# Hymba block on one core: half of the output weights split during attention and kept in DRAM, the gate's operands placed in weight buffers that are no longer used

## The chip, the cores and the metric

The kernel runs on one core of one Trainium2 chip. The metric is the device time of one execution in microseconds (us). The kernel before took 2211.99 us, the median of three runs (2210.46 to 2216.73).

## The reference

One layer of a streaming encoder, 2048 tokens of 1024 features in float32. A normalised input is projected once; 512 columns feed a state-space layer, the rest are q, k, v of a chunked attention with 8 heads. Both results are normalised, joined, and sent through one output projection; a SwiGLU feed-forward layer follows.

```python
h = rmsnorm(x, norm_mix_g[l])
proj = h @ w_in[l]
...
y = jax.nn.gelu(y.reshape(bsz, seq, D_SSM))
y = y * jax.nn.sigmoid(y @ w_glu.astype(f32) + b_glu.astype(f32))
...
y_att = chunked_attention(q, k, v, attn_rel_bias[l])
mixed = jnp.concatenate([rmsnorm(y_ssm, norm_ssm_out_g[l]),
                         rmsnorm(y_att, norm_att_out_g[l])], axis=-1)
x = x + mixed @ w_out[l]
h2 = rmsnorm(x, norm_ffn_g[l])
x = x + (jax.nn.silu(h2 @ w_gate[l]) * (h2 @ w_up[l])) @ w_down[l]
return rmsnorm(x, norm_final_g)
```

## The kernel before

**Precision.** Nearly every product is made of three matmuls (`mm3`): each float32 operand is split into a rounded part and a rest (`split`, L177 to L179). ScalarE (ACT) casts the rounded part, VectorE (DVE) subtracts it, so a split is one instruction on each of the two engines, the second waiting for the first. Names such as `gh`/`gl` or `woh`/`wol` are the two parts of one operand.

**Stages.** After a prologue (state-space layer, first projections) the attention runs as 130 steps in four blocks of 512 tokens. The order of work on TensorE (PE) is written out by hand and kept. In a step PE makes the scores of one head and query chunk (tiles `sc`), the transposes of the probabilities of two steps before (tiles `pt`), now and then the product with v (tiles `pj`, one `pv_head` per four steps), and "fillers": pieces of other work, written as Python generators with a first and a last step, that put matmuls (tiles `pf`) between the links of this chain. The chain of one step goes PE scores, DVE reduction with the bias (`mn`), ACT exponential (`s`), PE transposes (`pt`), ACT cast (`pth`, L956), DVE subtraction (`ptl`, L957), and the next `pt` reuses the bank. Work put `behind()` the chain (`issue_after(k.least)`) is issued on its engine only after the latest reduction.

**The mix phase** (`mix_phase`, L1088) is a generator, too. Its first 21 pieces (`MIX_N`) are fillers of steps 116 to 129, the rest follows attention. It holds, for each 512-token block sb: the sigmoid gate of the state-space half (`glu`: four output tiles f of four `mm3` groups each, from four operands `ys` split by `load`), the gain and inverse root of the two norms (`rstd1` with `newton` gives a row `b.o[c]`; `spread` (L146) broadcasts it over the partitions by four small PE transposes into a PSUM bank; `rstd2`, L1204, multiplies the four tiles `ya` or `ys` by it on DVE, reading that bank), and the product with `w_out`. While sb is multiplied, the gate of the next block (`nxt`) is made.

**Output weights.** `load_wo` (L1105) fetches rows of `w_out` 512 KB at a time: q = 4, 5 into `xt` during attention, q = 6, 7, 0, 1 into the `m` tiles and q = 2, 3 into `xt` behind it. `split_wo` splits all eight.

**Queues.** All loads named here go through the queue of SyncE (SP), which issues them in program order and stands still where one of them has to wait. SP also carries the stacked input weights of the attention fillers (`w<-wss`, L769, 1 MB each, three buffers `w`), the k and bias rows, and `fetch` (L1131): four loads `yr<-y` of the next two blocks' state-space outputs.

Of the kernel before, what the change touches and what calls it, by code (L numbers as in the profile page):

```python
# [10 lines left out]
F32R = mybir.dt.float32r  # L11
# [5 lines left out]
P = 128  # L17
# [715 lines left out]
def att_phase(k, ident, S, aw, x0, roots):  # L733

    tc, nc, io, pfs = k.tc, k.nc, k.io, k.pfs
    with ExitStack() as cx:
# [78 lines left out]
        def qk_unit(sb, pr):  # L815
# [12 lines left out]
            for c in range(2):  # L828
# [36 lines left out]
                yield  # L865

        QK_N = 1 + 2 * KT

# [147 lines left out]
        for sb in range(NSB):  # L1016
# [23 lines left out]
        for s in range(N + LAG + 2):  # L1040
# [9 lines left out]
            for o in TURNED.get(s % 32, ORDER) if s < N - 32 else ORDER:  # L1050
# [33 lines left out]

MIX_N = 21


def mix_phase(k, S, bank):  # L1088
# [3 lines left out]
    with ExitStack() as cx:  # L1092
# [10 lines left out]
        def load_wo(n, pool, tag, **kw):  # L1103
            raw = k.t(pool, tag, [P, 1024], **kw)
            nc.sync.dma_start(raw[:], io["w_out"][QS[n] * P : (QS[n] + 1) * P, :])  # L1105
            return raw

        def split_wo(raws):
            for n, q in enumerate(QS):
                W[q] = k.t(mx, f"woh{q}", [P, D], F32R), k.t(mx, f"wol{q}", [P, D], F32R)  # L1110
                raw = raws[n] if n < len(raws) else load_wo(n, wr, "xt")
                with tc.issue_after(k.last_root) if n > 1 else nullcontext():
                    split(k, W[q][0][:], W[q][1][:], raw[:])

# [16 lines left out]
        def fetch(sb):  # L1131
            yrs[0] = k.t(my, "yr", [P, 4, L, 128])
            for f in range(4):
                nc.sync.dma_start(yrs[0][:, f], S["y"][:, f * P : (f + 1) * P, sb * 64 : sb * 64 + 128].rearrange("j p t -> p j t"))  # L1134

        def take(sb):
# [6 lines left out]
            else:  # L1143
                yt = k.t(my, "ys", [P, 4, SB])
                b.ys = [yt[:, f] for f in range(4)]
            b.g = []
            if sb == 2:
# [10 lines left out]
        def load(b, f):  # L1158
            gh, gl = k.t(my, f"gh{f}", [P, SB], F32R), k.t(my, f"gl{f}", [P, SB], F32R)
            split(k, gh[:], gl[:], b.ys[f])  # L1160
            b.g.append((gh, gl))

# [6 lines left out]
        def glu(b, bank, late=False):  # L1169
# [5 lines left out]
            for f in range(4):  # L1175
                ps = bank()
                cs = slice(f * P, (f + 1) * P)
                for q in range(4):
                    mm3(te, ps[:, :512], Wg[q][0][:, cs], Wg[q][1][:, cs], b.g[q][0][:], b.g[q][1][:], q == 0, q == 3)
                    if q < 3:  # L1180
                        yield
# [77 lines left out]
        def pre_tiles():  # L1259
            while True:  # L1260
                for f in range(4):
                    for m in "hl":
                        yield k.t(my, f"g{m}{f}", [P, SB])
                t = k.t(my, "yr", [P, 4, L, 128])[:].rearrange("p a b c -> p (a b c)")
# [4 lines left out]
        b, nxt = take(0), take(1)  # L1269
        for f in range(4):  # L1270
            with tc.issue_after(k.least):
                load(b, f)
            yield
        g = glu(b, bank, True)
# [12 lines left out]
        for f in range(4):  # L1287
            load(nxt, f)
        yield

# [492 lines left out]
def block_kernel(tc, io, phases="pusamf"):  # L1783
# [3 lines left out]
    with ExitStack() as cx:  # L1787
# [4 lines left out]
        def pp():  # L1792
# [8 lines left out]
            "hq": k.t(dram, "hq", [2, F2, 7, P, 512]), "wc": k.t(dram, "wc", [F2, 7, P, 512]), "wt": k.t(dram, "wt", [4, P, HALF]),  # L1801
            "kt": k.t(dram, "kts", [CH, NG, 2, P]), "tm": k.t(dram, "tms", [P, NG, P]),
        }
# [87 lines left out]
```

## Time and profile before

| | |
|---|---|
| median of three runs | 2211.99 us |
| the profiled execution's own time | 2214.67 us |
| its span in the profile | 2212.9 us, so 1.8 us lie around it |
| PE busy | 97% of the span |
| mean granted clock | 0.992 |
| last product of attention with v begins, first gate matmul of the next block | 673.71 us, 677.76 us |
| first matmul with the output weights | 693.73 us |
| DMA | 431.20 MB, mean 195 GB/s |

A busy engine in the profile is one that has an instruction of arithmetic under way. The granted clock is the share of full TensorE speed that the chip allowed in a stretch. In a timeline a row gives start, duration, engine, line of the source, operation, output tile, input tile, and in brackets the idle time of the engine just before and what ended it.

### The profile page before, as it was taken

To read this page: it belongs to the slowest core of one execution; us is meant where nothing else is said; L and a number is where in the kernel's file an instruction comes from. 1 tells how busy PE (TensorE), PEld (TensorE's weight loads), DVE (VectorE), ACT (ScalarE), POOL (GpSimd) and SP (SyncE) were. 2 spreads that over 40 slices of the span, in tenths; PEclk is the share of its full clock that TensorE was granted. 3 is DMA by queue.
4 is the path that set the end of the run, shared out by engine and by line. 5 is a ranking of instruction groups with operands and counts; after the bars stand their busy time and mean duration, and the time that the engine had idled before them with its cause. 6 is when DMAs were issued, how large, how long until landed. Compare 5 with 4: busy or idle time off the path is not lost.

```text
span 2212.9 us, 30057 instructions
## 1 busy us (share of the span) xinstructions
PE 2155.7 (97%) x10606; PEld 1816.1 (82%) x10606; DVE 1534.3 (69%) x2667; ACT 1008.1 (46%) x1684; POOL 371.5 (17%) x839
## 2 busy tenths in 40 slices
PE   8999999999998999999999999999999999999998
PEld 6787898998977888788888887888888788888887
DVE  8767566565568657767776768767665477689785
ACT  6356566555677521533333345333333443354332
POOL 3367777676110000000000000000000100000000
PEclk9999999999999999999999999999999999999999
DMA  9788977665633346835555657545332395465552
GB/s 323 240 284 268 303 229 241 210 202 174 202 111 138 119 143 218 262 100 182 177 174 190 211 189 262 194 159 203 110 113 102 123 390 179 164 220 197 193 216 77
DMA packets 194423, 431.20 MB, mean 195 GB/s; under 512 B 19744, under 2 KB 37200, under 8 KB 187168
## 3 DMA queue, kind: packets, MB, share of 16 engines
q1 hardware_dynamic: 186448, 404.05, 54.7%
q0 software_dynamic: 7824, 25.24, 3.8%
q8 instruction: 83, 1.36, 0.3%
q14 instruction: 68, 0.56, 0.1%
HBM read 290.00 MB, written 131.10 MB: 190 GB/s over the span
## 4 chain that ended last, share of the span: by engine, by line
PE 61%; DMA 5%; DVE 2%; ACT 1%; issue 1%; SPq 0%; DVEq 0%; ACTq 0%
PE X L81 21%; PE ps L81 17%; PE Y L81 11%; PE big L81 6%; PE W L81 5%; DMA acc<-x 2%; DMA lo<-hc 1%; DMA x<-xt 1%; DVE xt L1239 0%; DMA hd<-wc 0%; DMA m<-in_w_out 0%; ACT hi L179 0%; DMA hc<-gh 0%; DVE acc L1664 0%; SPq L1134 0%
## 5 line engine op out<-in xcount | busy, mean ns | idle before, releaser
L81 PE MATMUL X<-hi,c 128*128 128x512 f32 x1408 | 451.7, 392 | 9.6 <-DVE c L179 5.0
L81 PE MATMUL ps<-hd,hd 128*128 128x512 f32 (+1 forms) x1920 | 428.8, 384 | 3.4 <-DVE hd L179 2.0
L81 PEld LDWEIGHTS ps<-hd,hd 128*128 128x128 f32 x1920 | 353.3, 188 | 75.1 <-DVE hd L179 2.7
L81 PEld LDWEIGHTS X<-hi,c 128*128 128x128 f32 x1408 | 265.8, 189 | 66.5 <-DVE c L179 5.9
L81 PE MATMUL X<-lo,c 128*128 128x512 f32 x704 | 275.3, 391 | 0.0
L179 ACT CAST hd<-hd 128x1536 fp32r<-128x1536 f32 (+1 forms) x106 | 147.5, 1394 | 230.7 <-DMA hd<-hq 164.9
L81 PE MATMUL Y<-hi,c 128*128 128x512 f32 x704 | 224.8, 390 | 1.5 <-DVE u L1526 1.5
L179 DVE TENSOR_TENSOR hd<-hd 128x1536 fp32r<-128x1536 f32 (+1 forms) x106 | 174.2, 1645 | 35.9 <-ACT hd L179 35.1
L179 DVE TENSOR_TENSOR c<-S,c 128x512 fp32r<-128x512 f32 x176 | 120.9, 688 | 101.0 <-ACT c L179 100.8
L1630 POOL DMA_DIRECT2D hd<-hq x7 | 5.2, 745 | 1072.0 <-PE X L81 1060.7
L1522 ACT COPY u<-X 128x512 f32<-128x512 f32 x132 | 77.4, 587 | 197.7 <-PE X L81 197.7
L179 ACT CAST c<-S 128x512 fp32r<-128x512 f32 x176 | 109.4, 622 | 121.7 <-PE Y L81 62.0
L81 PE MATMUL big<-m,woh 128*128 128x512 f32 x512 | 161.2, 396 | 0.0
L81 PEld LDWEIGHTS Y<-hi,c 128*128 128x128 f32 x704 | 132.7, 189 | 29.9 <-DVE u L1526 2.2
L1664 DVE TENSOR_TENSOR acc<-acc,ps 128x512 f32<-128x512 f32 x196 | 130.3, 683 | 38.5 <-PE ps L81 38.0
L81 PEld LDWEIGHTS X<-lo,c 128*128 128x128 f32 x704 | 132.9, 189 | 27.5
L179 ACT CAST c<-raw 128x512 fp32r<-128x512 f32 x132 | 82.2, 623 | 148.8 <-PE Y L81 73.0
L81 PE MATMUL pf<-hi,w 128*128 128x512 f32 x416 | 148.8, 410 | 0.0
L81 PE MATMUL Y<-lo,c 128*128 128x512 f32 x352 | 137.2, 390 | 0.0
L957 DVE TENSOR_TENSOR ptl<-pt,pth 128x640 fp32r<-128x640 f32 (+3 forms) x152 | 98.3, 646 | 46.1 <-ACT pth L956 42.1
L940 ACT ACTIVATE s<-s,mn 128x640 f32<-128x640 f32 (+4 forms) x128 | 97.9, 765 | 51.4 <-DVE mn L937 50.9
L956 ACT CAST pth<-pt 128x640 fp32r<-128x640 f32 (+3 forms) x152 | 83.8, 551 | 81.2 <-PE pt L84 75.7
(494 smaller groups left out, 4281.3 us busy)
## 6 DMA issues: line engine op xcount, KB each, us to landing
w<-wss SPq DMA_DIRECT2D x36, 1024.0 KB, 6.1
hq<-g SPq DMA_DIRECT2D x140, 256.0 KB, 2.1
hd<-hq SPq DMA_DIRECT2D x35, 768.0 KB, 4.4
hd<-wc SPq DMA_DIRECT2D x35, 768.0 KB, 5.9
raw<-in_w_gate SPq DMA_DIRECT2D x44, 512.0 KB, 3.6
raw<-in_w_up SPq DMA_DIRECT2D x44, 512.0 KB, 4.1
wc<-px SPq DMA_DIRECT2D x66, 256.0 KB, 3.1
wss<-w SPq DMA_DIRECT2D x12, 1024.0 KB, 6.3
```

Source lines behind the costliest of these rows:

```text
L81: return self.tc.keep_in_program_order(self.tc.nc.tensor.matmul(*a, **b))
L179: return nc.scalar.copy(hi, raw), nc.vector.tensor_tensor(lo, raw, f32(hi), op=ALU.subtract)
L940: nc.scalar.activation(s[:, :nk], s[:, :nk], AF.Exp, bias=mn[:], scale=-1.0, accum_out=sums[sb, pr][:, hh, qp : qp + 1])
L956: nc.scalar.copy(pth[:, a:b, qp, :], pt[:, a:b, :])
L957: k.low = nc.vector.tensor_tensor(ptl[:, a:b, qp, :], pt[:, a:b, :], f32(pth[:, a:b, qp, :]), op=ALU.subtract).ins
L1522: nc.scalar.copy(u[:], ps[:])
L1630: (nc.gpsimd if aside else nc.sync).dma_start(f32(lo), src.rearrange("g p c -> p g c"))
L1664: V.tensor_tensor(a, a, ps[:], op=ALU.add)
```

## The change

- A new unit `out_weights`, a filler of steps 58 to 69, loads w_out rows q = 0 to 3, splits each in two halves behind the attention chain (8 casts and 8 subtractions of 128x512), and stores both parts into a new DRAM tensor `wos` (16 stores of 256 KB).
- `split_wo` splits only q = 4 to 7. The parts of q = 0 to 3 come back as eight loads of 512 KB, ordered behind the last load of `w_out`. The four loads `yr<-y` are put behind these as well.
- The tag `w` joins the buffers that outlive attention. Two of the three `w` buffers hold the gate's operands (`k.G`, `gate_operand`), the third the tile `ys` of blocks 1 and 3.
- The four operand splits of block 0 move from the first four pieces of the mix phase into steps 116 to 119 (`HEADS`), one per step. `MIX_N` falls from 21 to 17, so the sixteen gate groups of block 0 are spread over ten steps instead of nine, and start earlier.
- The spread of block 0's attention norm moves from behind attention into the last piece before the last `pv_head`, and from a `big` tile into a `pf` bank; `rstd2` of it is issued there, too.

```diff
+WO = 58, 69
-LASTING = "hi0", "lo0", "hi1", "lo1", "hi2", "lo2", "xt", "raw"
+LASTING = "hi0", "lo0", "hi1", "lo1", "hi2", "lo2", "xt", "raw", "w"
+HEADS = 116, 117, 118, 119
...
+        def out_weights():
+            raws = {}
+
+            def load(n):
+                raws[n] = k.t(aw, "raw", [P, D], bufs=2)
+                nc.sync.dma_start(raws[n][:], io["w_out"][QS[n] * P : (QS[n] + 1) * P, :])
+
+            load(4)
+            load(5)
+            for i in range(8):
+                yield
+                n, hs = 4 + i // 2, slice(i % 2 * SB, i % 2 * SB + SB)
+                parts = [k.t(aw, f"{m}{i % DB}x", [P, SB], F32R) for m in ("hi", "lo")]
+                with behind():
+                    split(k, parts[0][:], parts[1][:], raws[n][:, hs])
+                for m in range(2):
+                    nc.sync.dma_start(S["wo"][n - 4, :, m, hs], f32(parts[m][:]))
+                if i % 2 and n < 6:
+                    load(n + 2)
+            yield
...
+        units.append(Unit(out_weights(), 9, *WO, 2))
...
+            if s == HEADS[0]:
+                k.G = [k.t(k.lp, "w", [P, 2, 1024], F32R, bufs=WB) for _ in range(2)]
+            if s in HEADS:
+                f = HEADS.index(s)
+                with behind():
+                    split(k, *gate_operand(k, f), k.ys[f])
...
-MIX_N = 21
+MIX_N = 17
...
-            for n, q in enumerate(QS):
+            for n, q in enumerate(QS[:4]):
...
+            for n, q in enumerate(QS[4:]):
+                W[q] = k.t(mx, f"woh{q}", [P, D], F32R), k.t(mx, f"wol{q}", [P, D], F32R)
+                for m in range(2):
+                    with tc.issue_after(k.last_wo):
+                        k.last_wo = nc.sync.dma_start(f32(W[q][m][:]), S["wo"][n, :, m]).ins
...
-        for f in range(4):
-            with tc.issue_after(k.least):
-                load(b, f)
-            yield
         g = glu(b, bank, True)
...
         for f in range(4):
             load(nxt, f)
+        pb = bank()
+        spread(k, te, pb, b.o[0], 0)
+        rstd2(b, 0, pb[:])
         yield
...
-        pb = bk()
-        spread(k, te, pb[:, :512], b.o[0], 0)
-        rstd2(b, 0, pb[:, :512])
         for n, _ in enumerate(glu(nxt, bk)):
...
-        raws += [load_wo(n, mx, f"m{QS[n + 2]}") for n in range(2, 6)]
+        raws += [load_wo(n, mx, f"m{QS[n + 2]}") for n in range(2, 4)]
```

**PE at steps 118 to 120.** These are PE's rows in the kernel before from the transposes of step 118 on; `gh` and `gl` are the gate's operand, `pf_8031` is the gate's first output tile.

```order
L84 MATMUL pt_7952<-ident_80,s_7863 128x128 x5
L81 MATMUL sc_7982<-k_1693_7796,q2h_7794 128x320
L81 MATMUL sc_7982<-k_1693_7796,q2l_7795 128x320
L81 MATMUL sc_7982<-k_1693_7796,q2h_7794 128x320
L81 MATMUL sc_7982<-k_1693_7796,q2l_7795 128x320
L84 MATMUL pt_7992<-ident_80,s_7894 128x128 x5
L81 MATMUL sc_8010<-k_1693_7796,q2h_7794 128x320
...
L84 MATMUL pt_8019<-ident_80,s_7948 128x128 x5
L81 MATMUL pf_8031<-gh_1725_7978,hi_1446_6558 128x512
```

In the changed kernel the operand is called `w_7913` or `w_7914` (both parts in one buffer, which is why two of a group's three matmuls read alike).

```order
L86 MATMUL pt_8017<-ident_81,s_7924 128x128 x5
L83 MATMUL pf_8043<-w_7913,hi_1467_6615 128x512 x2
L83 MATMUL pf_8043<-w_7913,lo_1468_6616 128x512
L83 MATMUL sc_8049<-k_1714_7853,q2h_7851 128x320
...
L86 MATMUL pt_8059<-ident_81,s_7957 128x128 x5
L83 MATMUL pf_8043<-w_7913,hi_1516_6847 128x512 x2
L83 MATMUL pf_8043<-w_7913,lo_1517_6848 128x512
L83 MATMUL pf_8043<-w_7914,hi_1575_7117 128x512 x2
L83 MATMUL pf_8043<-w_7914,lo_1576_7118 128x512
L83 MATMUL sc_8075<-k_1714_7853,q2h_7851 128x320
```

Between two transposes there stood scores alone; now a gate group stands in front of the scores of step 119, and two more behind its transposes.

**The end of attention, DVE and PE.** This is DVE in the kernel before, from the last `ptl` of attention to the norm's multiplications (`ya<-ya,ga,big`).

```order
L957 TENSOR_TENSOR ptl_8225<-pt_8302,pth_8224 128x5x128
L1183 TENSOR_SCALAR yr_7972<-pf_8284,bg_7968 128x8x64
L179 TENSOR_TENSOR gl_1804_8331<-ys_7973,gh_1803_8330 128x512
...
L1187 TENSOR_TENSOR raw_7423<-raw_7423,yr_7972 128x512 x2
L1123 TENSOR_TENSOR sq_8319<-sq_8319,sg_8321 128x512
L981 TENSOR_TENSOR ya_8203<-pj_8350,yt_8367 64x512
L1123 TENSOR_TENSOR sq_8319<-sq_8319,sg_8324 128x512
L990 TENSOR_TENSOR ya_8203<-ya_8203,pj_8370 128x512
L1123 TENSOR_TENSOR sq_8319<-sq_8319,sg_8327 128x512
L1204 SCALAR_TENSOR_TENSOR ya_1758_8115<-ya_1758_8115,ga_7967,big_8392 128x512
```

The same stretch of DVE in the changed kernel:

```order
L980 TENSOR_TENSOR ptl_8305<-pt_8362,pth_8304 128x5x128
L181 TENSOR_TENSOR w_7913<-w_8038,w_7913 128x512 x2
L181 TENSOR_TENSOR w_7914<-w_8038,w_7914 128x512 x2
L1243 SCALAR_TENSOR_TENSOR ya_1758_8099<-ya_1758_8099,ga_8032,pf_8389 128x512
L1226 TENSOR_TENSOR raw_7479<-raw_7479,yr_8037 128x512 x2
L1226 TENSOR_TENSOR raw_7480<-raw_7480,yr_8037 128x512 x2
L1163 TENSOR_TENSOR sq_8370<-sq_8370,sg_8372 128x512
L1243 SCALAR_TENSOR_TENSOR ya_1759_8100<-ya_1759_8100,ga_8032,pf_8389 128x512
L1163 TENSOR_TENSOR sq_8370<-sq_8370,sg_8375 128x512
L1243 SCALAR_TENSOR_TENSOR ya_1760_8101<-ya_1760_8101,ga_8032,pf_8389 128x512
L1163 TENSOR_TENSOR sq_8370<-sq_8370,sg_8378 128x512
L1243 SCALAR_TENSOR_TENSOR ya_1761_8102<-ya_1761_8102,ga_8032,pf_8389 128x512
```

And PE in the changed kernel over the same stretch, from the last transposes to the first gate group of the next block (`big_8444`):

```order
L86 MATMUL pt_8362<-ident_81,s_8327 128x128 x5
L86 MATMUL pf_8389<-ident_81,no_8259 128x128 x4
L83 MATMUL pj_8402<-pth_8304,v_1665_7568 128x512
...
L83 MATMUL pj_8402<-ptl_8305,v_1668_7571 128x128
L86 MATMUL pj_8422<-ident_81,rb_8400 128x128 x4
L83 MATMUL big_8444<-w_7913,hi_1467_6615 128x512 x2
```

The spread is the row `pf_8389<-ident_81,no_8259`; it stood behind `pj` as `big_8392<-ident_80,no_8248` before. The four multiplications that read it moved forward on DVE, in between the squares. As the kernels are built, `pf_8389` lies in PSUM bank 1, and the next gate tile `big_8444` takes banks 0 and 1; before, the spread lay in banks 0 and 1 and the first gate tile behind it in banks 6 and 7, the second in 4 and 5, where `pj` had been.

**SP at steps 58 to 69.** In the kernel before, the load `w_5088` (input weights of a coming filler) stands here:

```order
L583 DMA nba_98<-nbs_69 64x576
L769 DMA w_5088<-wss_74 128x2048
L861 DMA ks_68<-k_1007_4570 128x512
L861 DMA ks_68<-k_1010_4573 128x512
L826 DMA k_1141_5197<-ks_68 128x512
```

In the changed kernel the same load is called `w_5127`:

```order
L885 DMA wos_78<-hi0x_4984 128x512
L885 DMA wos_78<-lo0x_4985 128x512
L874 DMA raw_4990<-in_w_out 128x1024
L885 DMA wos_78<-hi1x_5054 128x512
L885 DMA wos_78<-lo1x_5055 128x512
L771 DMA w_5127<-wss_74 128x2048
L885 DMA wos_78<-hi2x_5131 128x512
```

It now stands behind the five rows above it, all of the new unit, and behind both `ks` stores, which it preceded.

More of the change, by code (lines that the diff above doesn't have):

```diff
@@ L1104, in load_wo @@
             raw = k.t(pool, tag, [P, 1024], **kw)
-            nc.sync.dma_start(raw[:], io["w_out"][QS[n] * P : (QS[n] + 1) * P, :])
+            k.last_wo = nc.sync.dma_start(raw[:], io["w_out"][QS[n] * P : (QS[n] + 1) * P, :]).ins
             return raw
         def split_wo(raws):
-            for n, q in enumerate(QS):
+            for n, q in enumerate(QS[:4]):
                 W[q] = k.t(mx, f"woh{q}", [P, D], F32R), k.t(mx, f"wol{q}", [P, D], F32R)
-                raw = raws[n] if n < len(raws) else load_wo(n, wr, "xt")
-                with tc.issue_after(k.last_root) if n > 1 else nullcontext():
-                    split(k, W[q][0][:], W[q][1][:], raw[:])
+                raw = raws[n]
+                split(k, W[q][0][:], W[q][1][:], raw[:])
+            for n, q in enumerate(QS[4:]):
[3 more added lines that the diff above has]
+                        k.last_wo = nc.sync.dma_start(f32(W[q][m][:]), S["wo"][n, :, m]).ins
         def squares(src):
@@ L1143, in take @@
             else:
-                yt = k.t(my, "ys", [P, 4, SB])
-                b.ys = [yt[:, f] for f in range(4)]
-            b.g = []
+                if sb == 1:
+                    k.y1 = k.t(k.lp, "w", [P, 4, SB], bufs=WB)
+                b.ys = [k.y1[:, f] for f in range(4)]
             if sb == 2:
@@ L1158, in load @@
         def load(b, f):
-            gh, gl = k.t(my, f"gh{f}", [P, SB], F32R), k.t(my, f"gl{f}", [P, SB], F32R)
-            split(k, gh[:], gl[:], b.ys[f])
-            b.g.append((gh, gl))
+            split(k, *gate_operand(k, f), b.ys[f])
         def load_a(b, sb):
@@ L1260, in pre_tiles @@
             while True:
-                for f in range(4):
-                    for m in "hl":
-                        yield k.t(my, f"g{m}{f}", [P, SB])
+                for _ in range(2):
+                    t = k.t(k.lp, "w", [P, 4, SB], bufs=WB)
+                    for i in range(4):
+                        yield t[:, i]
                 t = k.t(my, "yr", [P, 4, L, 128])[:].rearrange("p a b c -> p (a b c)")
```

11 lines of the change are left out of this document (7 added, 4 removed).

## The prediction

> **What bounds the kernel now.** I read the page first, then the windows of 10 us around the end of attention, then the timelines of PE, DVE, ACT and SP in the windows that lose time. The page's first part and its chain of waits:
>
> ```profile
> PE 2155.7 (97%) x10606; PEld 1816.1 (82%) x10606; DVE 1534.3 (69%) x2667; ACT 1008.1 (46%) x1684; POOL 371.5 (17%) x839
> ...
> PE 61%; DMA 5%; DVE 2%; ACT 1%; issue 1%; SPq 0%; DVEq 0%; ACTq 0%
> ```
>
> PE is the bound. The change leaves its matmuls as they are, so it can give or take only time in which PE stands still or runs at a lower clock. Where that is near the edits, the windows say (stretch, PE's possible and busy time, then PEld, DVE, ACT and POOL, the granted clock, DMA share and GB/s):
>
> ```profile
> 630.00:640.00 10.00, 7.61 (x45) 6.26 (x43) 6.23 (x11) 8.98 (x15) 5.69 (x5) 0.97 0.20 44
> 640.00:650.00 10.00, 9.39 (x45) 8.44 (x46) 6.16 (x13) 7.19 (x15) 0.07 (x1) 0.69 0.86 312
> ...
> 680.00:690.00 10.00, 7.86 (x32) 6.09 (x30) 9.94 (x16) 6.62 (x11) 0.59 (x1) 0.83 0.88 270
> 690.00:700.00 10.00, 7.05 (x31) 5.23 (x32) 7.30 (x21) 7.64 (x11) 0.00 (x0) 1.00 0.97 386
> ```
>
> PE loses 2.4 us at 630 and 0.6 at 640, where the clock is also at 0.69, so 0.31 x 9.39 = 2.9 us more. It loses 2.1 at 680 with the clock at 0.83 (0.17 x 10 = 1.7), and 2.95 at 690. That is some 12.7 us, and nothing the change does can give more than that plus the small waits between.
>
> **The gate's operands (first loss).** PE's timeline at step 119, with the wait in brackets, and DVE's:
>
> ```profile
> 636.87 0.42 PE L81 MATMUL sc<-k,q2h 128*128 128x320 f32 x1 [0.38 <-DVE mn L937]
> 637.59 0.41 PE L81 MATMUL sc<-k,q2h 128*128 128x320 f32 x1 [0.16 <-DVE k L857]
> 640.04 1.33 PE L84 MATMUL pt<-ident,s 128*128 128x128 f32 x5 [1.89 <-DVE ptl L957]
> 643.01 1.33 PE L84 MATMUL pt<-ident,s 128*128 128x128 f32 x5 [0.57 <-DVE ptl L957]
> ```
>
> ```profile
> 636.85 1.41 DVE L857 TENSOR_TENSOR k<-pf,k 64x512 fp32r<-64x512 f32 x2
> 638.29 0.84 DVE L179 TENSOR_TENSOR gl<-raw,gh 128x512 fp32r<-128x512 f32 x1
> 639.16 0.82 DVE L957 TENSOR_TENSOR ptl<-pt,pth 128x640 fp32r<-128x640 f32 x1
> ```
>
> The subtraction `gl` stands between the last k rows and `ptl`, and PE has no filler at this step, since the gate groups need the operands that are being made. The change makes them at steps 116 to 119 and puts a group in front of step 119's scores and two behind its transposes. So the 1.89 and 0.57 go, and with them the slow clock: 1.89 + 0.57 + 2.9 = 5.4 us. The 0.38 and 0.16 lie under the new groups: 0.5 more. Against it, sixteen groups over ten steps leave three steps with one group less. A group is worth about 0.7 us of cover (three matmuls some 0.23 apart), so these steps may wait 0 to 2.1 us longer; small waits on `ptl` are there already, and I take 0.7. Net: **-5.2 us**, bounds -6 and -3 (the lower gain if half of the wait stays, as `ptl` can come only 0.84 us earlier than now).
>
> **The spread in a bank that the next tile needs (the new loss).** DVE behind the last `ptl`, and PE over the same time:
>
> ```profile
> 673.69 0.82 DVE L957 TENSOR_TENSOR ptl<-pt,pth 128x640 fp32r<-128x640 f32 x1 [1.51 <-ACT pth L956]
> ...
> 675.09 2.49 DVE L179 TENSOR_TENSOR gl<-ys,gh 128x512 fp32r<-128x512 f32 x4
> 677.61 2.50 DVE L1187 TENSOR_TENSOR raw<-raw,yr 128x512 f32<-128x512 f32 x4
> 680.02 0.68 DVE L1123 TENSOR_TENSOR sq<-sq,sg 128x512 f32<-128x512 f32 x1
> ...
> 683.26 2.72 DVE L1204 SCALAR_TENSOR_TENSOR ya<-ya,ga,big 128x512 f32<-128x512 f32 x4
> ```
>
> ```profile
> 677.40 0.60 PE L84 MATMUL big<-ident,no 128*128 128x128 f32 x4
> 677.76 0.48 PE L81 MATMUL big<-gh,hi 128*128 128x512 f32 x1
> ...
> 682.89 0.47 PE L81 MATMUL big<-gh,hi 128*128 128x512 f32 x1 [2.14 <-DVE ya L990]
> ```
>
> Now PE goes from `pj` over the spread to the first gate tile without a wait and stops before the second, whose banks held `pj`, until `ya<-ya,pj`. In the changed kernel the first gate tile covers bank 1, where the spread lies until the fourth `ya<-ya,ga,pf` has read it. By DVE's order, four subtractions, four `raw<-raw,yr`, three `sq` and the four multiplications stand between the last `ptl` and that point: 2.49 + 2.50 + 3 x 0.68 + 2.72 = 9.75 us. PE needs from the end of `ptl` (about 674.43, when DVE's next instruction starts) to the end of `pj` (677.40) 3.0 us. So it stands still for 9.75 - 3.0 = **+6.8 us**; 5.8 if the instructions overlap at their ends as the starts in the rows do, 8.0 if a square has to wait for ACT. The old 2.14 goes, since `pj` is evacuated long before the second tile is due, and its slow clock: **-2.1 and -1.7**. The spread's 0.36 us (677.40 to 677.76) move into the wait for the last `ptl`: **-0.4**, at worst 0.
>
> A wait that long lowers the clock afterwards. What it costs, the trace shows twice at 2 us of wait: 1.7 us at 680 to 690, and here (PE's row, then two windows of 4 us):
>
> ```profile
> 500.75 1.32 PE L84 MATMUL pt<-ident,s 128*128 128x128 f32 x5 [2.16 <-DVE ptl L957]
> ```
>
> ```profile
> 500.00:504.00 4.00, 3.25 (x10) 2.77 (x11) 3.18 (x6) 1.89 (x4) 3.61 (x5) 0.50 0.86 242
> 504.00:508.00 4.00, 4.00 (x18) 3.51 (x17) 0.83 (x2) 1.04 (x3) 1.21 (x2) 0.71 0.73 187
> ```
>
> Half of 3.25 and 0.29 of 4.00 make 2.8 us, with the head of it up to 3.2. Between 1.7 and 3.2 I take **+2.4**.
>
> [...]
>
> **Output weights (third loss).** PE, ACT and SP:
>
> ```profile
> 698.49 0.50 PE L81 MATMUL big<-m,wol 128*128 128x512 f32 x1 [2.78 <-DVE wol L179]
> ```
>
> ```profile
> 692.52 1.05 ACT L179 CAST woh<-m 128x1024 fp32r<-128x1024 f32 x1 [2.18 <-DMA m<-in_w_out]
> ```
>
> ```profile
> 653.09 0.32 SPq L991 DMA_DIRECT2D ya_s<-ya  x1
> 680.25 4.76 SPq L1134 DMA_DIRECT2D yr<-y  x4
> 685.06 3.32 SPq L1105 DMA_DIRECT2D m<-in_w_out  x4
> ```
>
> PE waits for the split of q = 6, which waits for a load that SP could issue only behind four `yr` loads that took it 4.76 us. After the change the two loads left stand directly behind `ya_s<-ya`, and land during attention. The splits that remain are then done while PE still multiplies gates: **-2.8 us**. The eight loads of `wos` (4 MB against the 2 MB of rows that they replace) come when `pj` frees their place, at a few hundred GB/s within some 14 us; PE asks for q = 0 only behind the first four q. The `yr` loads come later by these, and their reader is the gate of block 2, over 20 us on. Both cost nothing; if that cover were gone, each us late is one on PE.
>
> **Steps 58 to 69.** Eight casts and eight subtractions of the size of `gl`, so some 5 us on ACT and 5.4 on DVE, and 6 MB more for the DMA. The windows and, for the load named in the order of SP, its issue, the landings of its kind there, the DVE row next to which the `lo1x` subtraction now stands, and PE's first use:
>
> ```profile
> 370.00:390.00 20.00, 19.90 (x137) 18.43 (x136) 12.72 (x24) 11.52 (x23) 17.57 (x60) 1.00 0.77 252
> 390.00:410.00 20.00, 20.00 (x137) 18.57 (x136) 10.17 (x20) 8.94 (x19) 7.04 (x9) 1.00 0.60 174
> ```
>
> ```profile
> 378.75 0.33 SPq L769 DMA_DIRECT2D w<-wss  x1
> ```
>
> ```profile
> DMA to landing us min/median/max: 5.8/6.1/9.1
> ```
>
> ```profile
> 386.03 0.81 DVE L937 CUSTOM_DVE_ANT_0 s<-sc,nbb 128x640 f32<-128x640 f32 x1
> ```
>
> ```profile
> 400.69 0.48 PE L81 MATMUL pf<-hi,w 128*128 128x512 f32 x1
> ```
>
> SP now issues this load only when the subtraction behind 386.03 is stored, at about 387.6 instead of 378.75. With 9.1 us it lands at 396.7, 4.0 us ahead of its use; the k and bias rows queued behind it have as much. DVE is at 0.6 and ACT at 0.5 there, PE is full. So the price lies between 0 and 4 us (a `ptl` pushed back by up to 0.7 at each of a few splits); I take **+0.5**, near the full windows.
>
> **The sum**, against the profiled execution's own 2214.67: -5.2 - 2.1 - 1.7 - 0.4 + 6.8 + 2.4 - 2.8 + 0.5 = -2.5, so 2212.2. That execution lies 2.7 above the median of 2211.99, so the median to expect is **2209.5**. With all bounds one way: -6 - 2.1 - 1.7 - 0.4 + 5.8 + 1.7 - 2.8 = -5.5, or -3 - 2.1 - 1.7 + 8.0 + 3.2 - 2.8 + 4 = +5.6; so 2206.5 to 2217.6.
>
> **Rivals.**
> - The bank does not hold PE back, or hardly (the multiplications come sooner, or the first gate tile need not wait). Then 6.8 and 2.4 fall out: -11.7, 2200.3. DVE's order and the shared bank speak against it; the size of the three losses speaks for a gain once this term shrinks. 0.25, partial cases with it.
> - The first gain does not come: four casts and subtractions at 116 to 119 collide there as they do at 119 now. Without the 5.2: +2.7, 2214.7. For it: `behind` placed the present ones, too, and ptl was late nevertheless. Against it: fillers stand at those steps. 0.10.
> - Slower by the new unit. A subtraction in front of `ptl` that makes PE wait 2.16 us and lowers the clock costs 2.16 + 3.2 = 5.4 us, as at 500.75. The DVE is 0.6 busy, and POOL at 17.57 of 20 at the same time. From two of the eight splits on it decides: -3.0 + 10.8 = +7.8, 2219.8. Against it: no wait of PE stands in these windows now. 0.20.
> - The forecast itself: 0.45.
>
> A measurement of this kernel can tell about 0.3%, 6.6 us, from no change. Faster by more than that: the first rival, 0.25. Slower: the third and a fifth of the second, 0.22. Within: 0.53. The range that leaves out 2 in 10 reaches into both outer rivals: 2200 to 2220.
>
> **What would show it.** Right: in the profile after, no wait of about 1.9 us and no lower clock near 640; one wait of 6 to 8 us of the first `big` gate matmul, for the multiplication of `ya` on DVE; no wait for `wol`; PE full between 370 and 410. Wrong: that one wait under 3 us, a clock under 0.9 around steps 116 to 119, waits for `w` or `ptl` from 360 to 420, or a new wait on `wos` loads behind 690.

## The result and the profile after

The changed kernel took 2210.35 us (median of 17 runs, 2204.38 to 2214.17), the kernel before beside it 2216.73 us (17 runs, 2210.37 to 2220.13). The ratio is 0.9975, 95% interval 0.9966 to 0.9983: 5.5 us faster (3.8 to 7.5), inside the 0.3% that the prediction called no change. The profiled execution after took 2205.35 us, near the low end of its runs, against 2214.67 before: the two profiles differ by 9.3 us where the typical runs differ by some 6. So about 3 us between the two profiles is chance.

The engines' busy time in the changed kernel:

```profile
PE 2146.7 (97%) x10606; PEld 1810.2 (82%) x10606; DVE 1534.4 (70%) x2671; ACT 1005.5 (46%) x1686; POOL 374.1 (17%) x839
```

The same 10606 matmuls are busy for 9.0 us less (2155.7 before). A matmul at a lower clock is busy for longer (the product with `wol` 0.63 us in a slow stretch before, 0.39 in the same place after, 729.68 and 726.86 in the rows further down), and the mean granted clock rose from 0.992 to 0.996, so nearly all that the two profiles differ by is clock that came back; the waits gone and the waits new come out about even (57.2 us of PE's span before, 56.9 after). The windows around the end of attention (the stretch and its length, the busy time of PE, PEld, DVE, ACT and POOL, then the granted clock, DMA share and GB/s):

```profile
630.00:640.00 10.00, 8.86 (x55) 7.58 (x54) 6.92 (x12) 8.49 (x13) 5.33 (x5) 1.00 0.21 42
640.00:650.00 10.00, 9.73 (x61) 8.48 (x59) 8.65 (x17) 7.98 (x15) 0.00 (x0) 1.00 0.88 309
670.00:680.00 10.00, 3.30 (x21) 2.71 (x20) 9.97 (x17) 7.77 (x11) 0.00 (x0) 0.93 0.57 181
680.00:690.00 10.00, 10.00 (x33) 8.03 (x34) 7.15 (x10) 4.96 (x7) 0.59 (x1) 0.73 0.70 270
690.00:700.00 10.00, 10.00 (x50) 8.38 (x49) 8.75 (x25) 6.64 (x11) 0.00 (x0) 1.00 1.02 309
```

At 630 to 650 PE now does 116 matmuls instead of 90, at full clock throughout (0.69 before at 640). At 690 PE is full: the wait for `wol` is gone. In their place stands a hole at 670 to 680, where PE works for 3.30 of 10 us, and a low clock behind it (0.73 at 680 to 690). PE's rows of the two places:

```profile
639.50 0.76 PE L86 MATMUL pt<-ident,s 128*128 128x128 f32 x5 [1.02 <-DVE ptl L980]
...
679.96 1.19 PE L83 MATMUL big<-w,hi 128*128 128x512 f32 x2 [6.34 <-DVE ya L1243]
```

And DVE's rows behind the last `ptl` of attention:

```profile
669.73 0.82 DVE L980 TENSOR_TENSOR ptl<-pt,pth 128x640 fp32r<-128x640 f32 x1 [0.93 <-ACT pth L979]
670.47 2.49 DVE L181 TENSOR_TENSOR w<-w,w 128x512 fp32r<-128x512 f32 x4
672.88 0.74 DVE L1243 SCALAR_TENSOR_TENSOR ya<-ya,ga,pf 128x512 f32<-128x512 f32 x1
673.54 2.49 DVE L1226 TENSOR_TENSOR raw<-raw,yr 128x512 f32<-128x512 f32 x4
...
679.07 0.74 DVE L1243 SCALAR_TENSOR_TENSOR ya<-ya,ga,pf 128x512 f32<-128x512 f32 x1
```

PE had finished `pj` at 673.62 (679.96 less the 6.34 of the bracket). It stands until the fourth multiplication, at 679.07, has read the spread's bank; ahead of that one on DVE stand operand splits and gate products that nobody yet waits for.

Where the time went, from the same landmark of both profiles (us from the start; a difference that grows more negative is a gain):

| landmark on PE | before | after | difference |
|---|---|---|---|
| transposes at step 112, ahead of the moved splits | 617.60 | 617.93 | +0.33 |
| last transposes of attention | 672.16 | 668.21 | -3.95 |
| first matmul with the output weights | 693.73 | 694.48 | +0.75 |
| spread of the second norm, first block | 708.15 | 705.36 | -2.79 |
| the same, last block | 888.99 | 882.22 | -6.77 |
| end of the span | 2212.9 | 2203.6 | -9.3 |

So the operands gained 4.3 us, the end of attention lost 4.7, the output weights gained 3.5, and then something that the prediction has no term for gained 4.0 between 708 and 889, where the change adds no work to PE and takes none from it. One gate group of about 0.7 us stood behind the last transposes before (at 672.68) and stands ahead of them now; counted with the operands, they gained 5.0 and the end of attention lost 5.4. Another 2.5 us come behind 889: 1.4 of them in waits at the start of the feed-forward part (4.90 us before, 3.51 after; 3.3 in a second profile of the kernel before, so within chance).

### The profile page after: what moved, and what is told of

Same layout as the page of the kernel before. It is cut to its first block, busy times and chain, and to the rows that moved or that the text cites. A ratio compares the mean times of both kernels' runs of the same rounds, so it can differ in the third digit from the quotient of the medians.

```text
span 2203.6 us, 30105 instructions
## 1 busy us (share of the span) xinstructions
PE 2146.7 (97%) x10606; PEld 1810.2 (82%) x10606; DVE 1534.4 (70%) x2671; ACT 1005.5 (46%) x1686; POOL 374.1 (17%) x839
## 4 chain that ended last, share of the span: by engine, by line
PE 80%; DVE 6%; DMA 5%; POOL 4%; issue 3%; ACT 2%; SPq 0%; DVEq 0%; ACTq 0%; POOLq 0%
PE X L83 21%; PE ps L83 20%; PE Y L83 11%; PE pf L83 8%; PE big L83 7%; PE W L83 5%; PE pj L83 3%; PE pt L86 2%; PE sc L83 2%; DVE lo L181 1%; POOL X L646 1%; POOL st L643 1%; POOL X L645 1%; DMA x<-xt 1%; POOL st L644 1%
```

## The experiments

Ratios are to the kernel before, run beside each experiment. The theory had three parts: the shared bank holds PE for the 6.34 us; the moved operands are worth some 4 to 5; the wait for `wol` went because its loads no longer stand behind `yr`. The rivals were that the first gate matmul waits for something else (its operand, or ACT), that the gain up to the end of attention is chance in the clock, and that the wait for `wol` depends on the number of splits.

**spread_behind**: the changed kernel with only the spread and `rstd2` of block 0 back where they were.

```diff
-        pb = bank()
-        spread(k, te, pb, b.o[0], 0)
-        rstd2(b, 0, pb[:])
         yield
...
+        pb = bk()
+        spread(k, te, pb[:, :512], b.o[0], 0)
+        rstd2(b, 0, pb[:, :512])
```

> The changed kernel, with one part undone: the spread of block 0's attention norm and its four multiplications stand behind attention in a `big` tile again. Theory (the bank): the 6.3 us wait of the first gate matmul for the multiplication of ya goes, and the old wait of about 2.1 us of the second gate tile comes back; net 4 us faster than the changed kernel, more if the clock stays up behind the shorter wait, so 2204 to 2206 beside a before of 2216.7, ratio near 0.995. Rival (the first gate matmul waits for the subtractions of its operand anyway, the bank does not matter): the wait stays at 5 us or more, ratio 0.9975 as for the changed kernel.

Measured: 2202.99 us (6 runs, 2198.38 to 2206.64), ratio 0.9940 (0.9927 to 0.9953), some 7.8 us faster than the changed kernel by the ratios. PE's longest wait between the last transposes and the output weights, and the window that had a clock of 0.73:

```profile
678.44 0.70 PE L83 MATMUL big<-w,hi 128*128 128x512 f32 x2 [1.45 <-DVE ya L1013]
```

```profile
680.00:690.00 10.00, 10.00 (x50) 8.38 (x49) 10.00 (x18) 9.32 (x14) 0.00 (x0) 1.00 0.99 357
```

The first gate tile starts at 674.00 without a wait. The old wait is back, 1.45 us long, for the evacuation of `pj`, and the clock stays at 1.00. From the last transposes to the first matmul with the output weights it is 19.27 us (26.27 in the changed kernel, 21.57 before). The bank's part of the theory holds: the moved spread cost 7.0 us of path.

**mults_first**: the spread stays in its early place and its bank, but its four multiplications go ahead of the operand splits on DVE.

```diff
-        for f in range(4):
-            load(nxt, f)
         pb = bank()
         spread(k, te, pb, b.o[0], 0)
-        rstd2(b, 0, pb[:])
+        with tc.high_priority():
+            rstd2(b, 0, pb[:])
+            for f in range(4):
+                load(nxt, f)
```

> The changed kernel, with the four multiplications of ya put on DVE directly behind the last ptl, and the four subtractions of the next gate operand behind them; the spread keeps its bank. Theory (the bank): the fourth multiplication ends 2.7 us behind the last ptl, before pj ends (3.0), so the first gate matmul hardly waits (under 0.7 us, for a subtraction); next in line is the third gate tile, whose banks held pj and which may wait up to 2.5 us for ya<-ya,pj. Net 4 to 6 us faster than the changed kernel, ratio 0.995 or lower. Rival (the wait has another cause, such as the operand or ACT): 5 us or more of waiting stay at the first gate matmul, ratio 0.9975.

Measured: 2201.40 us (6 runs, 2199.71 to 2205.73), ratio 0.9935 (0.9922 to 0.9949): the fastest median here, though the interval does not tell it from spread_behind. So moving the spread early, with its readers in front, earned nothing that these runs can show; with its readers behind other work it cost. DVE's rows behind the last `ptl`, then PE's wait:

```profile
672.99 0.82 DVE L980 TENSOR_TENSOR ptl<-pt,pth 128x640 fp32r<-128x640 f32 x1 [0.93 <-ACT pth L979]
673.73 2.71 DVE L1243 SCALAR_TENSOR_TENSOR ya<-ya,ga,pf 128x512 f32<-128x512 f32 x4
676.36 2.49 DVE L181 TENSOR_TENSOR w<-w,w 128x512 fp32r<-128x512 f32 x4
```

```profile
684.05 0.70 PE L83 MATMUL big<-w,hi 128*128 128x512 f32 x2 [1.40 <-DVE ya L1013]
```

The same instructions, the same bank, another order on one engine: the multiplications end at 676.4, before PE is through `pj`, and the 6.34 us are gone. So it is not the amount of DVE work that held PE but what stood ahead of the last reader of the bank. The operand's subtractions now end later (at 678.85) without holding the first gate matmul, so that rival falls.

**operands_late**: the changed kernel with the operand splits of block 0 back in the pieces of the mix phase.

```diff
-            if s in HEADS:
-                f = HEADS.index(s)
-                with behind():
-                    split(k, *gate_operand(k, f), k.ys[f])
...
-MIX_N = 17
+MIX_N = 21
...
+        for f in range(4):
+            with tc.issue_after(k.least):
+                load(b, f)
+            yield
         g = glu(b, bank, True)
```

> The changed kernel, with the gate's operands of block 0 split in the first four pieces of the mix phase again, and the gate groups where they were before. Theory (the operands collide at step 119): a wait of about 1.9 us for ptl with a lower clock comes back near 640 us, and the last transposes of attention start 4 us later than in the changed kernel; 4 us slower than it, ratio near 0.9993. Rival (the gain up to the end of attention comes from chance in the clock): no such wait, time as the changed kernel, 0.9975.

Measured: 2216.79 us (12 runs, 2207.13 to 2219.29), ratio 0.9999 (0.9989 to 1.0010), 5.3 us slower than the changed kernel by the ratios. The profiled execution (2207.13) is the fastest of the twelve, so only the place is read from it. PE and the window:

```profile
641.21 0.77 PE L86 MATMUL pt<-ident,s 128*128 128x128 f32 x5 [1.75 <-DVE ptl L980]
...
643.61 1.33 PE L86 MATMUL pt<-ident,s 128*128 128x128 f32 x5 [0.82 <-DVE ptl L980]
```

```profile
640.00:650.00 10.00, 7.97 (x32) 6.93 (x33) 7.00 (x14) 6.34 (x13) 0.00 (x0) 0.66 0.71 228
```

The waits and the low clock (0.66; 0.69 before) are back as a pair. From the transposes near 618 to the last ones it takes 55.47 us against 50.28: the operands are worth 5.2 us, as the prediction had it.

**order_only**: the kernel before, with one thing of the change: the `yr` loads go behind the loads of `w_out`.

```diff
...
+                with tc.issue_after(k.last_m):
                     nc.sync.dma_start(yrs[0][:, f], S["y"][:, f * P : (f + 1) * P, sb * 64 : sb * 64 + 128].rearrange("j p t -> p j t"))
```

> The kernel before, with only the order of loads behind attention changed: the loads of w_out stand ahead of the four yr loads. Theory (PE waits for wol because the loads of q = 6 and on stand behind yr): the 2.8 us wait for wol is gone or under 0.5 us without any stored weights, ratio near 0.9987. Rival (it takes the smaller number of splits, as DVE and ACT set the time): the wait stays above 2 us, ratio 1.000.

Measured: 2210.01 us (12 runs, 2208.15 to 2216.24), ratio 0.9974 (0.9966 to 0.9983). The time is as good as that of the whole change, but not for the expected reason: the wait for `wol` is still 1.93 us. PE, ACT and DVE:

```profile
698.04 0.50 PE L81 MATMUL big<-m,wol 128*128 128x512 f32 x1 [1.93 <-DVE wol L179]
```

```profile
692.25 2.94 ACT L179 CAST woh<-m 128x1024 fp32r<-128x1024 f32 x3
```

```profile
696.70 0.15 DVE L118 SCALAR_TENSOR_TENSOR no<-nf,ny 128x4 f32<-128x4 f32 x1
696.77 2.35 DVE L179 TENSOR_TENSOR wol<-m,woh 128x1024 fp32r<-128x1024 f32 x2
```

ACT no longer waits for a load (2.18 us before). The subtraction still starts only at 696.77, behind the inverse root of the norm (`no`, L118), which the program puts ahead of the later splits on DVE. So the load's lateness was worth 0.85 us of the 2.78; the rest was DVE's order. Only some 2 us of waits went, yet the kernel gained 6: no stretch of low clock (a fall of the clock, below) is left between 684 and 850, of which the kernel before has three (near 684, 729 and 784: 0.83 in 680 to 690, 0.91 in 720 to 740 and 0.91 in 774 to 792; order_only has 1.00 in the last two, and behind 684.91 its matmuls of 512 columns start 0.23 us apart).

**order_and_root**: order_only, and the splits of q = 6 and 7 no longer put behind that root.

```diff
-                with tc.issue_after(k.last_root) if n > 1 else nullcontext():
+                with tc.issue_after(k.last_root) if n > 3 else nullcontext():
```

> The kernel before, with the loads of w_out ahead of the yr loads, and the splits of q = 6 and 7 no longer held behind the inverse root of the second norm. Theory (after the load order, the 1.9 us wait for wol that is left comes from DVE's order, in which the root of ten small steps stands ahead of wol): the wait for wol is under 0.3 us; 2 us faster than the run with the order alone, ratio near 0.9965, and no stored weights are needed for the third loss. Rival (ACT and DVE are short of time for eight splits): a wait for wol of 1.5 us or more remains or moves to a later q, ratio 0.9974 or higher.

Measured: 2212.36 us (12 runs, 2208.72 to 2216.55), ratio 0.9985 (0.9976 to 0.9995): no better than order_only, and by the ratios 2.4 us behind it. The `wol` wait is gone, and this is in its place, with a fall of the clock behind it (0.72 in 720 to 732, 1.00 there in order_only); DVE's rows ahead of it follow:

```profile
724.10 1.87 PE L81 MATMUL big<-ones,sq 128*128 128x1 f32 x8 [2.94 <-DVE nv L110]
```

```profile
716.20 2.49 DVE L179 TENSOR_TENSOR gl<-raw,gh 128x512 fp32r<-128x512 f32 x4 [5.06 <-ACT gh L179]
...
723.28 0.69 DVE L1248 TENSOR_TENSOR sa<-sa,xt 128x512 f32<-128x512 f32 x1 [3.45 <-ACT xt L1244]
```

The wait moved; it did not go, as the rival had it. Its reason was that ACT and DVE are short of time for eight splits. For DVE these rows show the contrary: it stood idle for 5.06 and 3.45 us behind ACT just before `nv`. ACT had been held up too, 1.45 and 0.54 us by the loads `ya<-ya_s`, and 2.12 us in its square of `xt` by the store of that tile. Counted from the start, PE arrives there 4.3 us earlier than in order_only, this chain only 1.6 us earlier; so PE now has to wait for it.

**no_store**: mults_first without the new unit and the stored halves: all eight splits stand behind attention again, with the loads and the root ordered as in order_and_root.

```diff
-        units.append(Unit(out_weights(), 9, *WO, 2))
...
-            for n, q in enumerate(QS[:4]):
+            for n, q in enumerate(QS):
...
+                raw = raws[n] if n < len(raws) else load_wo(n, wr, "xt")
+                with tc.issue_after(k.last_root) if n > 3 else nullcontext():
+                    split(k, W[q][0][:], W[q][1][:], raw[:])
...
```

> The changed kernel without stored weights: no unit at steps 58 to 69, all eight rows of w_out loaded and split behind attention with the loads ahead of yr, the splits of q = 4 to 7 not held behind the root, and the four multiplications of ya directly behind the last ptl as in the run with them first. Theory (the unit costs 1.6 to 2.7 us and what it saves can be had from the order alone): no wait for wol and none at 360 to 400 us; 1 to 3 us faster than the run with the multiplications first (2201.4), ratio 0.992 to 0.993. Rival (the stored halves relieve DVE and ACT where PE would wait): a wait for wol or for a later gate of 2 us or more behind 690 us, time 2201 to 2205, ratio 0.9935 to 0.995.

Measured: 2208.13 us (5 runs, 2204.41 to 2211.65), ratio 0.9962 (0.9949 to 0.9974), 6.0 us behind mults_first by the ratios, and slower than even its rival had forecast. PE's two longest waits behind the first matmul with the output weights and up to 730:

```profile
707.72 0.49 PE L83 MATMUL big<-m,woh 128*128 128x512 f32 x1 [0.79 <-ACT m L181]
...
722.13 1.36 PE L83 MATMUL big<-ones,sq 128*128 128x1 f32 x8 [3.30 <-DVE nv L112]
```

Behind the 3.30 us the clock falls to 0.50 (724 to 728); mults_first has 0.26 us at this product and no fall (1.00 in 720 to 740). So against this order of the splits the halves made during attention are worth some 6 us, net of what their making costs. It is the order of order_and_root, with the same wait at the same product; order_only's was 2.4 us better there. With that one the halves may be worth less, which no run tests.

**unit_only**: the kernel before, with only the unit `out_weights` added. What it stores is read by nobody.

```diff
...
+        units.append(Unit(out_weights(), 9, *WO, 2))
...
```

> The kernel before, with the new unit of steps 58 to 69 added alone: it loads, splits and stores q = 0 to 3, and nothing reads what it stores. Theory (the subtractions of the unit stand ahead of ptl and of the copies of U): PE waits of about 0.3, 0.6 and 0.8 to 1.7 us appear near 363, 373 and 387 us, 1.6 to 2.7 us in all, and nothing else changes; ratio near 1.001. Rival (the forecast's 0.5 us: the unit is hidden and those waits come from the other edits): no wait of PE between 355 and 425 us, ratio 1.000. Second rival (6 MB more crowd the DMA queues): waits for w or k near 400 us, 4 us and more, ratio 1.002 or higher.

Measured: 2217.31 us (11 runs, 2213.03 to 2219.54), ratio 1.0001 (0.9992 to 1.0011). In the profile PE has two new waits:

```profile
375.53 0.77 PE L85 MATMUL pt<-ident,s 128*128 128x128 f32 x5 [0.62 <-DVE ptl L979]
...
389.58 0.77 PE L85 MATMUL pt<-ident,s 128*128 128x128 f32 x5 [1.57 <-DVE ptl L979]
```

2.2 us together, without a lower clock (1.00 in 370 to 390 and in 390 to 410), of which the time of whole runs shows nothing beyond its interval (-1.8 to +2.4 us). The rival that priced such waits at 5.4 us each, with the clock, falls.

**before_again, order_again, after_again**: a second profile of the kernel before, of order_only and of the changed kernel, unaltered. They ask whether the falls of the clock behind 708 belong to a kernel or to one execution. For order_only and the changed kernel the author expected that they belong to the kernel, with no more than one fall each.

> The kernel before, profiled once more. Theory (part of the scatter of single runs is the clock, which falls after some stretches of low activity and not after others): the waits of PE stand at the same places with the same lengths within 0.3 us, while the stretches with a clock under 0.95 differ from the first profile in at least one of 500, 684, 728 and 785 us, at 1.5 us or so each. Rival (the clock follows the program alone): the same stretches fall again.

> The run with the load order alone, profiled once more. [...] Rival (the first profile of it was a chance): two or three falls, as in the kernel before.

> The changed kernel, profiled once more. [...]

Measured: 2215.52, 2207.19 and 2204.56 us. The changed kernel's PE row and window, and then the window of the kernel before, second profile:

```profile
682.86 1.19 PE L83 MATMUL big<-w,hi 128*128 128x512 f32 x2 [6.35 <-DVE ya L1243]
```

```profile
720.00:740.00 20.00, 19.75 (x100) 16.61 (x99) 14.95 (x46) 7.09 (x11) 0.00 (x0) 1.00 0.39 132
```

```profile
720.00:740.00 20.00, 19.75 (x93) 16.46 (x92) 13.58 (x44) 4.91 (x8) 0.00 (x0) 0.91 0.30 105
```

The wait for `ya` repeats to 0.01 us; others do not (`wol` 2.78 and 3.12 us in the kernel before; 2.7 and 1.3 us in all at steps 58 to 69 of the changed one, where 1.6 to 2.7 had been expected of the second). Behind 708 the falls repeat by kernel: two of them (near 729 and 784, 0.91 in 720 to 740 and in 774 to 792) in the first profile of the kernel before and three (near 845 as well, 0.86 in 840 to 852) in the second; none in either profile of the changed kernel; none in either of order_only (1.00 in these windows). The four places named for before_again fell again (near 728 and 785 the same 0.91 in both profiles), so that theory was wrong and its rival right there. Elsewhere the falls do not repeat: near 908 the changed kernel's first profile has one (0.50 in 908 to 912, a group of three matmuls takes 1.28 us) and its second none (0.69 us, 911.12 to 911.81).

**ten_more**: the kernel before with ten extra products ahead of its third output tile, whose results the tile overwrites; 2.3 us of work that puts all that follows later by as much.

```diff
+                    for _ in range(10 if (sb, i, n, c) == (0, 4, 0, 0) else 0):
+                        te.matmul(ps[:, :512], W[q][0][:, fc], b.m[q][0], start=True, stop=True)
```

> The kernel before, with ten matmuls 128x512 more than needed (each is overwritten by the next) in front of the first group of the third output tile, near 709 us: 10 x 0.228 = 2.3 us of added PE work, and nothing else. In three profiles of the program without them the two groups of one-column matmuls of the norms near 727, 782 and 842 us were followed by a clock of half speed 8 times of 9, for some 1.6 us each. [...] Rival (low activity lowers the clock wherever it stands): the falls stay, 2.3 us slower, ratio 1.001.

Measured: 2216.48 us (12 runs, 2214.10 to 2221.73), ratio 1.0005 (0.9996 to 1.0015). Two of the falls are gone (1.00 in 720 to 740 and in 838 to 852), one near 787 stays (0.86 in 780 to 790), and a new one has come behind a longer wait for `wol`:

```profile
700.20 0.50 PE L81 MATMUL big<-m,wol 128*128 128x512 f32 x1 [3.69 <-DVE wol L179]
```

```profile
700.00:710.00 10.00, 9.63 (x34) 7.50 (x35) 9.79 (x13) 5.78 (x10) 0.00 (x0) 0.83 0.21 71
```

The author's guess was that the moment at which the one-column products stand decides whether the clock falls behind them: at most one of the three falls left and, at some 1.6 us each, 2.5 us faster in all. The rival had 2.3 us slower. The time lies between the two, so this run decides nothing: 2.3 us of added work cost about 1 us (-0.9 to +3.3), which fits falls that went, but a new one came as well. The longer wait and the fall behind it stand ahead of the added products, which begin near 711.80, so these did not cause them.

## Why the prediction was right, and where it was not

- **The number.** That 2209.5 stands so near the measured 2210.35 is luck. The forecast was a gain of 2.5 us on a median of 2211.99, and beside the changed kernel the kernel before took 2216.73. The gain was 5.5 us, about twice the forecast; two terms were off, in opposite directions (the last two below).
- **That PE's lost time is all there is to win.** Right in kind, wrong in where: the prediction drew up PE's lost time from the windows of 630 to 700 and has no row for the clock behind them.
- **Operands, -5.2.** Right: 4.3 between the profiles, 5.2 to 5.3 by operands_late. The 1.89 us wait became 1.02 rather than nothing. The 0.7 us allowed for longer waits elsewhere did not come: the other waits up to the last transposes make 1.8 us in both profiles. The gate group that moved ahead of the landmark hides another 0.7 us of gain.
- **The bank, +6.8, and the clock behind it, +2.4.** Right: 6.34 us, and 0.07 x 3.30 + 0.27 x 10.00 = 2.9 us of clock. DVE's order was foreseen; that one multiplication ran early (672.88) does not matter, as the fourth decides. spread_behind and mults_first show the mechanism from two sides.
- **The old wait and its clock, -3.8, and the spread, -0.4.** Right as far as the rows go: with the four terms together, last transposes to output weights, forecast +5.0, measured 26.27 - 21.57 = +4.7.
- **The output weights, -2.8.** The size was right (3.5 between the landmarks, of which 2.95 were the two waits for `wol`, 2.78 and 0.17), the cause only in part. The step said that PE waits for the split of q = 6 because its load is stuck behind the `yr` loads. order_only takes that away and wins 0.85 of the 2.95; the other 2.10 (1.93 and 0.17) stand behind the root on DVE. The changed kernel's `split_wo` also drops the rule that held the splits of q = 6 and 7 behind that root, which neither the list of changes nor the prediction mentions; order_and_root shows that this takes the rest of the wait away, and that with eight splits behind attention another wait comes instead. That none came in the changed kernel goes with the four splits that left this stretch (no_store); which of their loads, casts and subtractions made the room was not tested.
- **Steps 58 to 69, +0.5.** Mis-sized: the changed kernel's profile has waits of 0.37, 0.62 and 1.74 us there, 2.7 in all (1.3 in its second profile, where the 1.74 is 0.72). The prediction looked at the subtraction on DVE and at a load of weights; in the longest of the three, what was late was ACT. Its rows, then DVE's and PE's, of the changed kernel:

```profile
384.22 0.62 ACT L181 CAST hi1x<-raw 128x512 fp32r<-128x512 f32 x1 [3.12 <-DMA raw<-in_w_out]
...
385.26 0.58 ACT L1003 COPY yt<-pj 64x512 f32<-64x512 f32 x1
```

```profile
385.88 0.68 DVE L1004 TENSOR_TENSOR ya<-pj,yt 64x512 f32<-64x512 f32 x1 [3.64 <-ACT yt L1003]
386.59 0.83 DVE L980 TENSOR_TENSOR ptl<-pt,pth 128x640 fp32r<-128x640 f32 x1
```

```profile
387.47 0.77 PE L86 MATMUL pt<-ident,s 128*128 128x128 f32 x5 [1.74 <-DVE ptl L980]
```

```profile
370.00:390.00 20.00, 17.64 (x117) 15.90 (x117) 14.41 (x27) 11.39 (x23) 17.65 (x57) 1.00 0.94 303
```

  The new cast waits 3.12 us for its own load. The copy `yt` stands behind it on ACT and starts only at 385.26, DVE's `ya` waits 3.64 us for that copy, and `ptl` stands behind `ya`. PE's wait follows the load's: ACT waits 3.12, 2.95 (unit_only) and 2.10 us (after_again) for this load, and PE 1.74, 1.57 and 0.72 us, 1.38 less each time. The DMA share rose from 0.77 to 0.94: the prediction counted the 6 MB as covered because the engines had room, and did not ask whether a load would land before ACT reached its cast.
- **The term that was missing.** Behind 708 the prediction had nothing. PE's rows of the kernel before, and of the changed kernel, behind the one-column products of the norm (`ones,sq`) of the first block:

```profile
726.13 1.05 PE L81 MATMUL big<-ones,sq 128*128 128x1 f32 x8 [0.26 <-DVE nv L110]
...
728.83 1.05 PE L81 MATMUL big<-m,woh 128*128 128x512 f32 x2
729.68 0.63 PE L81 MATMUL big<-m,wol 128*128 128x512 f32 x1
730.11 1.05 PE L81 MATMUL big<-m,woh 128*128 128x512 f32 x2
```

```profile
723.35 1.05 PE L83 MATMUL big<-ones,sq 128*128 128x1 f32 x8 [0.26 <-DVE nv L112]
...
726.41 0.61 PE L83 MATMUL big<-m,woh 128*128 128x512 f32 x2
726.86 0.39 PE L83 MATMUL big<-m,wol 128*128 128x512 f32 x1
727.09 0.61 PE L83 MATMUL big<-m,woh 128*128 128x512 f32 x2
```

  The same wait of 0.26 us, the same products; but before, a group of three takes 1.28 us (728.83 to 730.11), and after, 0.68 (726.41 to 727.09). The first window before shows it as clock (720 to 740, then 774 to 792), and so does the window after:

```profile
720.00:740.00 20.00, 19.75 (x93) 16.45 (x92) 13.60 (x44) 4.85 (x7) 0.00 (x0) 0.91 0.35 120
774.00:792.00 18.00, 17.75 (x82) 14.81 (x81) 9.19 (x38) 2.90 (x4) 0.00 (x0) 0.91 0.42 146
```

```profile
720.00:740.00 20.00, 19.75 (x100) 16.64 (x99) 15.91 (x48) 6.32 (x10) 0.00 (x0) 1.00 0.41 138
774.00:792.00 18.00, 17.75 (x94) 14.98 (x93) 11.68 (x41) 2.91 (x4) 0.00 (x0) 1.00 0.38 136
```

  0.09 x 19.75 = 1.8 us and 0.09 x 17.75 = 1.6 us, two or three times per execution before, not once after. The visible terms with their measured sizes are -4.3 + 4.7 - 3.5 + 2.7 = -0.4; two or three of these falls are -3.4 to -5.2 more, so -3.8 to -5.6, and 5.5 was measured. That sum fits; that the falls account for the rest is argued from profiles, as no run takes away the falls alone.

What stays open: why these falls keep to a kernel. order_only has them neither time and gains 6 us with 2 us of waits, and ten_more did not settle whether the moment alone decides. Nor is it clear which part of the change takes them away here: order_only does, and unit_only still has all three (0.89 in 732 to 740, 0.91 in 774 to 792, 0.86 in 840 to 852). It is not that the new order of work is proof against them: spread_behind and mults_first, which run the same work behind 708 as the changed kernel, have one each, near 774 and 777 (0.97 and 0.91 in 774 to 792).

## What to carry to other kernels

Before moving a small tile into a bank that a large tile will need next, look at the order in which the other engine reads it: the same tile in the same bank cost 6.3 us with its readers behind other work, and nothing with them in front (mults_first, 2201.40 us, 0.9935 of before). A split that is moved under cover has to be covered on both of its engines and in its load: a cast that waits for its load on ACT passed that wait on to all that stood behind it there (3.12 us, of which 1.74 reached PE). And when the clock is part of the loss near a change, look at the clock in the whole span, not only in the windows of the edit.

## What the runs showed of the hardware

**The same wait may or may not lower the clock.** The prediction quoted a wait of 2.16 us at 500.75 and a clock of 0.50 and 0.71 behind it. The changed kernel has the same wait at the same step:

```profile
502.58 0.77 PE L86 MATMUL pt<-ident,s 128*128 128x128 f32 x5 [2.16 <-DVE ptl L980]
```

```profile
500.00:504.00 4.00, 1.84 (x11) 1.44 (x12) 3.94 (x7) 0.62 (x1) 3.90 (x5) 1.00 0.83 292
504.00:508.00 4.00, 4.00 (x24) 3.56 (x23) 1.77 (x6) 2.00 (x5) 2.69 (x4) 1.00 1.04 278
```

The clock stays at 1.00. The second profile of the changed kernel has a wait of 2.15 us at this step and a fall behind it: a clock of 0.79 and 0.78 from 504 to 512. So the 2.8 us that this fall cost before are part of the chance between the two first profiles. The 2.13 us wait of order_only at 684.91 was followed by no fall either (matmuls of 512 columns start 0.23 us apart behind it), while one of 2.14 us at 682.89 before was (0.43 us apart from 683.97 on, 0.83 in 680 to 690).

**How long a slow stretch is, and what it follows.** Three slow stretches in the first profile of the kernel before are 3.3 to 3.4 us long. They end at 687.31, 786.35 and 1363.08 us, read where the starts of matmuls of 512 columns go back from some 0.43 to 0.23 us apart. A lower clock followed waits of 1.89 to 2.16 us at three places of the kernel before (0.69 in 640 to 650 behind 1.89 us, 0.83 in 680 to 690 behind 2.14, 0.50 and 0.71 from 500 to 508 behind 2.16) and did not follow the 2.16 and 2.13 us above, nor the 2.78 us for `wol` at 698.49 in the kernel before (1.00 from 690 to 706). In the kernel before it also followed some 2.1 us of one-column products, during which PE counts as busy in the profile (0.91 in 720 to 740); in the changed kernel it did not (1.00 there). That the moment decides is the author's guess and was not shown; no run placed a wait at a chosen moment.
